# Gathered experts: all dots before all sums, and V tiles 70 to 127 as three products of split halves

## The chip, the cores and the metric

One core of one Trainium2 chip runs the whole two-block network in one launch. The metric is device microseconds of that launch; of several runs the median counts. Engines: PE (TensorE, matmuls), PEld (its weight loads), DVE (VectorE), ACT (ScalarE), POOL (GpSimd, which issues the gathers), SP (SyncE, which issues the plain loads). The sixteen DMA engines serve both queues.

## The reference, cut to what matters

The change lies in the last part, the PEER layer of the second block. Each of 512 tokens has 128 chosen experts (8 heads, 16 each) out of 16384; expert `e` has a row `peer_u[e]` and a row `peer_v[e]` of 1024 floats.

```
def chunk(args):
    hc, ec, gc = args
    u = peer_u[ec]
    a = jax.nn.gelu(jnp.einsum("ckd,cd->ck", u, hc).astype(jnp.float32)) * gc
    vv = peer_v[ec]
    return jnp.einsum("ck,ckd->cd", a.astype(vv.dtype), vv)
```

The result is added to `x`, and the sum is normalised (rmsnorm) to give the output.

## The kernel before, in words

`peer` (L1463) treats the four token tiles of 128 in two ways at once. Tiles 2 and 3 (`DT`, 256 tokens) are dense: every expert's value is computed. Tiles 0 and 1 (`GT`) are gathered: only the chosen rows are fetched.

Dense. The 16384 experts are 128 tiles of 128. `u_tile(n)` (L1721) loads a 512 KB tile of `peer_uT`, makes eight float32 matmuls with the tokens `hd` and writes gelu of the result by ACT into a slot of `big` (L1706; 94 slots `NS`, the first 50 in one tile, the other 44 in a second that `rest_of_big` makes at U tile 50; expert tile n has slot n mod 94). `gates` (L1731) multiplies slots by the gates, for expert tiles 0 to 15, 16 to 79 and 80 to 127 (`parts`) in turn: for eight tokens at a time DVE makes one-hot factors in float16 (L1759, L1760, L1764), PE multiplies them (L1748), and DVE multiplies the slots by the product (L1752). `v_tile(n)` (L1772) loads 512 KB of `peer_v` and makes four float32 matmuls (eight records in the trace: a float32 matmul here shows as two), 128 x 128 by 128 x 512, from slot n into four PSUM banks.

Gathered. `row` (L1795) is one indirect DMA issued by POOL: 128 rows of 4 KB, one for each token, into a ring of twelve buffers (`rtile`). `dots(t, s0, s1)` (L1801) gathers a column of `peer_u` and reduces its product with the tokens `h3` by one DVE instruction. `factors(t)` (L1808) makes gelu times gate of the 128 dots of each token and transposes it. `v_rows` (L1815) gathers four columns of `peer_v`; `v_sum` (L1818) copies four factors into a diagonal window by ACT (L1821) and adds the rows by eight matmuls (16 records at L1825). `last_norm(t)` (L1832) adds `x`, normalises and stores. `gather_units` (L1843) is the order of this work: dots of tile 0; then the 32 sums of tile 0 with four dots of tile 1 behind each of them; then the 32 sums of tile 1. A gather counts as one unit, so a dot is one and a sum four: 512 units in all.

The order of both. `seq` (L1875) has 256 steps: U tiles 0 to 93, then V and U tiles by turns (V0, U94, V1, ... V33, U127), then V34 to V127; so V tile n is step 94 + 2n up to n = 33 and step 128 + n from there. After each step, `fill` issues units: 1.4 a step for the first 50 steps, 2.3 from there on. `issue_after` puts the PE instructions of a unit behind the step's last matmul. DVE, ACT and POOL have no such tie: a planner lays each engine's queue in order of its own estimates of when operands are there, and on the chip each queue runs in that order. Wherever a part's V tiles begin, what is left of its gates is issued first (L1889).

`split` (L81) is used elsewhere: ACT copies a float32 tile into float32r (the high half), DVE subtracts it (the low half). `mm3` (L133) then makes three float32r matmuls: high by high, high by low, low by high.

Of the kernel before, what the change touches and what calls it, by code (L numbers as in the profile page):

```python
# [8 lines left out]
F32 = mybir.dt.float32  # L9
F32R = mybir.dt.float32r  # L10
# [10 lines left out]
S, D, NT, KD = 512, 1024, 4, 8  # L21
# [10 lines left out]
class Kern:  # L32
# [1430 lines left out]
    def peer(self):  # L1463
        nc, tc, A = self.nc, self.tc, self.A
        tt, ts, stt = nc.vector.tensor_tensor, nc.vector.tensor_scalar, nc.vector.scalar_tensor_tensor
        act = nc.scalar.activation
        GT, DT, DW = (0, 1), (2, 3), 256
        NS, NA = 94, 50
        parts = [0, 16, 80, 128]
        TB = 8  # L1470
        GS = 32768.0
        with ExitStack() as ctx:
            pb = ctx.enter_context(tc.tile_pool(name="pb", bufs=1, reuse_waits="tile"))
# [4 lines left out]
            def pu(shape=(128, 512)):  # L1478
                return pp.tile(list(shape), F32, tag="u", name=self.nm("pu"), bufs=2)

            def pw(shape=(128, 512)):
                return pp.tile(list(shape), F32, tag="w", name=self.nm("pw"), bufs=4)

            def pr(shape=(128, 512)):
                return pp.tile(list(shape), F32, tag="r", name=self.nm("pr"), bufs=2)

            def load(src, shape):

                raw = wp.tile([128] + shape, F32, tag="raw", name=self.nm("raw"))
                nc.sync.dma_start(raw[:], src)  # L1490
                return raw
# [9 lines left out]
            gp = [pb.tile([128, DW], F16, name=f"gp{j}") for j in range(2)]  # L1501
            hd = [pb.tile([128, 4, DW], F32, name=f"hd{j}") for j in range(2)]
            lctx = ctx.enter_context(ExitStack())
            lv = lctx.enter_context(tc.tile_pool(name="plv", bufs=1, reuse_waits="tile"))
            v = [lv.tile([128, 8, 2, 16], F32, name=f"pv{t}") for t in range(NT)]
            ix = [lv.tile([128, 8, 2, 16], U32, name=f"pix{t}") for t in range(NT)]
# [101 lines left out]
            with ExitStack() as c2:  # L1608
# [12 lines left out]
                for t in range(NT):  # L1621
                    tb = slice(t * 128, t * 128 + 128)
                    for j in range(2):
                        x = self.xn[t][j]
# [48 lines left out]
            def picks():  # L1673
# [9 lines left out]
                for t in DT:  # L1683
# [10 lines left out]
                    gT = wk.tile([128, 128], F32, tag="gT", name=self.nm("gT"))  # L1694
                    ts(gT[:], p[:, 2, :], GS, None, op0=OP.mult)
                    nc.vector.tensor_copy(gp[0][:, sl], gT[:])
# [9 lines left out]
            big = [bp.tile([128, NA, DW], F32, name="big")]  # L1706

            def slots(n0, n1):

                while n0 < n1:  # L1710
                    i = n0 % NS
                    b, i, w = (0, i, NA) if i < NA else (1, i - NA, NS - NA)
                    m = min(n1, n0 + w - i)
                    yield n0, m, big[b], i
                    n0 = m

            def slot(n):
                _, _, b, i = next(slots(n, n + 1))
                return b[:, i, :]

            def u_tile(n):  # L1721

                p = pu()
                raw = load(A["peer_uT"][n].rearrange("p (k e) -> p k e", k=8), [8, 128])
                for k in range(KD):
                    self.u_last = nc.tensor.matmul(p[:, :DW], raw[:, k, :], hd[k // 4][:, k % 4, :], start=k == 0,  # L1726
                                                   stop=k == KD - 1)
                self.gelu = act(slot(n), p[:, :DW], AF.Gelu_apprx_tanh)  # L1728
                self.pace = self.u_last

            def gates(n0, n1, psum):  # L1731

                w, g = n1 - n0, TB // 2

                def by2(x, t0, w):
                    return x[:, t0:t0 + TB].rearrange("p (g i) -> p g i", i=2)[:, :, None, :].to_broadcast([128, g, w, 2])

                made = []  # L1740

                def products():
                    t0, o2, og = made.pop(0)
                    p = psum([128, TB, w])
                    with tc.issue_after(self.pace.ins):
                        for i in range(TB):
                            for j in range(2):
                                nc.tensor.matmul(p[:, i, :], o2[:, i // 2, :, i % 2], og[j][:, i // 2, :, i % 2], start=j == 0,  # L1748
                                                 stop=j == 1)
                    for n, m, b, i in slots(n0, n1):  # L1750
                        b = b[:, i:i + m - n, t0:t0 + TB]
                        stt(b, p[:, :, n - n0:m - n0].rearrange("p t n -> p n t"), 1.0 / GS, b, op0=OP.mult, op1=OP.mult)  # L1752

                for t0 in range(0, DW, TB):
                    if len(made) == 2:
# [12 lines left out]
                while made:  # L1768
                    products()
                    yield  # L1770

            def v_tile(n, acc):  # L1772
                raw = load(A["peer_v_2"][n * 128:n * 128 + 128, :], [D])
                a = slot(n)
                for t, c in itertools.product(range(2), range(2)):
                    self.pace = nc.tensor.matmul(acc[t][c][:], a[:, t * 128:t * 128 + 128], raw[:, c * 512:c * 512 + 512],  # L1776
                                                 start=n == 0, stop=n == 127)

            def rest_of_big():
                lctx.close()  # L1780
                bq = ctx.enter_context(tc.tile_pool(name="pbig2", bufs=1, reuse_waits="tile"))
                big.append(bq.tile([128, NS - NA, DW], F32, name="big2"))


            ga_t = [ga.tile([128, 128], F32, name=f"ga{t}") for t in GT]
# [9 lines left out]
            def row(src, idx):  # L1795
                u = rtile("u")
                nc.gpsimd.indirect_dma_start(out=u[:], out_offset=None, in_=A[src],  # L1797
                                             in_offset=bass.IndirectOffsetOnAxis(ap=idx, axis=0))
                return u

            def dots(t, s0, s1):  # L1801
                for s in range(s0, s1):
                    u = row("peer_u_2", ei[t][:, s:s + 1])
                    nc.vector.tensor_tensor_reduce(u[:], u[:], h3[t][:], scale=1.0, scalar=0.0, op0=OP.mult, op1=OP.add,  # L1804
                                                   accum_out=ga_t[t][:, s:s + 1])
                    yield 1

            def factors(t):  # L1808
                act(ga_t[t][:], ga_t[t][:], AF.Gelu_apprx_tanh)
                tt(ga_t[t][:], ga_t[t][:], gg[t][:], op=OP.mult)  # L1810
                p = pu([128, 4, 128])
                nc.tensor.transpose(p[:, 0, :], ga_t[t][:], self.ident[:])
                act(aT[t][:].rearrange("p g r -> p (g r)"), p[:, 0, :], AF.Copy)

            def v_rows(t, r):  # L1815
                return [row("peer_v_2", eT[t][:, 32 * g + r:32 * g + r + 1]) for g in range(4)]
# [25 lines left out]

            def gather_units():  # L1843

                yield from dots(0, 0, 128)
                factors(0)
                for t in GT:
                    acc = [pr(), pr()]
                    us = v_rows(t, 0)
                    yield 4  # L1850
                    for r in range(32):
                        nx = v_rows(t, r + 1) if r < 31 else None
                        v_sum(t, r, us, acc)
                        yield 4 if r < 31 else 0
                        us = nx
                        if t == 0:
                            yield from dots(1, 4 * r, 4 * r + 4)
                    if t == 0:
                        factors(1)
                    last_norm(t, acc)  # L1860

            units = gather_units()
# [20 lines left out]
            acc, gt, todo, room = None, None, 0, 0.0  # L1883
            nbatch = DW // TB

            for j, (kind, n) in enumerate(seq):
                if kind == "v" and n == 0:
                    acc = [[pw() for _ in range(2)] for _ in range(2)]
                if kind == "v" and n in parts and gt is not None:  # L1889
                    for _ in gt:  # L1890
                        pass
                    gt = None
                if kind == "u":
                    if n == NA:
                        for _ in picks:
                            pass
                        rest_of_big()
                    if n % 3:
                        next(picks, None)
                    u_tile(n)  # L1900
                else:
                    v_tile(n, acc)
                if gt is not None:
                    todo += rate
                    while todo >= 1:
                        todo -= 1
                        next(gt, None)
                if (kind, n) in start:
                    i = start[kind, n]
                    gt, todo = gates(parts[i], parts[i + 1], pu if i else pw), 0.0  # L1910

                    rest = seq.index(("v", parts[i])) - j - 1
                    rate = (nbatch + 2) / (rest - 1)

                room = fill(room + (1.4 if acc is None and n < NA else 2.3))
# [90 lines left out]
```

## Time and profile before

| what | value |
|---|---|
| median of 3 runs | 2919.87 us (2919.39 to 2923.93) |
| the profiled execution | 2930.82 us, its span 2929.1 us |
| PE busy | 2717.2 us (93%) |
| DVE busy | 1848.5 us (63%) |
| ACT busy | 1019.7 us (35%) |
| POOL busy | 723.5 us (25%) |
| mean granted PE clock | 0.972 |
| HBM read | 736.90 MB, mean 257 GB/s over the span |
| V tiles on PE (L1776) | 1024 records, 471.4 us |
| sums on PE (L1825) | 1024 records, 126.4 us |
| dots on DVE (L1804) | 256, 311.3 us |

Busy time is added up over instructions, and PE's records overlap their neighbours by some 0.16 us; the pace of a row of matmuls is read from the distance of their starts. A group in the timeline gives start, length, engine, line, operation and, in brackets, the idle time before it with what ended it. V tile 0 starts at 2125.64 us, and the last matmul ends at 2919.7 us.

### The profile page before, as it was taken

The numbers are of one execution on the slowest core, as the hardware profiler recorded it, in microseconds if no ns is written. First come the engines' busy times: TensorE is split into PE (matmuls) and PEld (weight loads), VectorE is DVE, ScalarE is ACT, GpSimd is POOL, SyncE is SP. The second block draws the span as 40 slices with busy tenths as digits, with TensorE's granted clock in tenths as the row PEclk, the third lists the DMA queues.
The fourth block names the chain that finished last, engine by engine and source line by source line (L and its number), as shares of the span: only waits on it lengthen the run. The fifth ranks groups of instructions, "written<-read, shape, count | busy, mean of one in ns | idle before, by whom it ended". The sixth has DMA issues, their size and how long they took to land.

```text
span 2929.1 us, 38343 instructions
## 1 busy us (share of the span) xinstructions
PE 2717.2 (93%) x13730; PEld 1907.3 (65%) x13730; DVE 1848.5 (63%) x3907; ACT 1019.7 (35%) x1672; POOL 723.5 (25%) x679
## 2 busy tenths in 40 slices
PE   7999969999999879999999889989989898699998
PEld 4776757777777667766678778877745554244333
DVE  5562569998888858998535399968557522452001
ACT  5442348777777653445633332200100000000000
POOL 1000050000000110101000343566543444444440
PEclk9999979999999989999999999999999999899999
DMA  7226568989999842322222348899988899999995
GB/s 258 87 86 215 206 212 324 355 319 354 351 351 348 317 148 86 108 72 66 89 91 94 119 166 284 335 409 409 360 326 318 327 362 350 324 355 360 369 375 184
DMA packets 228689, 752.10 MB, mean 257 GB/s; under 512 B 28160, under 2 KB 28448, under 8 KB 228496
## 3 DMA queue, kind: packets, MB, share of 16 engines
q1 hardware_dynamic: 145936, 458.69, 43.7%
q0 software_dynamic: 81984, 289.89, 27.1%
q8 instruction: 109, 1.79, 0.3%
q10 hardware_dynamic: 576, 1.05, 0.1%
q14 instruction: 84, 0.69, 0.1%
HBM read 736.90 MB, written 16.81 MB: 257 GB/s over the span
## 4 chain that ended last, share of the span: by engine, by line
PE 40%; DVE 9%; DMA 7%; issue 6%; POOL 2%; ACT 1%; DVEq 0%; another core or an unknown queue 0%; POOLq 0%; SPq 0%; ACTq 0%
PE pw L1776 12%; DMA u<-in_peer_u_dram,ei 6%; PE pu L1726 4%; PE pm L136 4%; PE pm L138 4%; PE pm L137 4%; PE pr L1825 3%; POOL u L1797 2%; DVE u L1804 2%; PE pa L1305 2%; DVE cv L1236 1%; PE pu L1748 1%; PE po L1334 1%; PE pw L138 1%; PE pw L136 1%
## 5 line engine op out<-in xcount | busy, mean ns | idle before, releaser
L84 DVE TENSOR_TENSOR lo<-raw,hi 128x1024 fp32r<-128x1024 f32 (+1 forms) x580 | 624.4, 1107 | 234.3 <-ACT hi L83 214.0
L83 ACT ACTIVATE hi<-raw 128x1024 fp32r<-128x1024 f32 (+1 forms) x600 | 556.9, 952 | 445.1 <-PE pm L137 197.0
L1804 DVE CUSTOM_DVE_ANT_0 u<-u,h 128x1024 f32<-128x1024 f32 x256 | 311.3, 1226 | 305.3 <-DMA u<-in_peer_u_dram,ei 258.7
L1726 PE MATMUL pu<-hd,raw 128*128 128x256 f32 x2048 | 474.1, 390 | 17.4 <-issue 8.3
L1776 PE MATMUL pw<-raw,big 128*128 128x512 f32 x1024 | 471.4, 609 | 6.7 <-DVE big L1752 6.7
L1726 PEld LDWEIGHTS pu<-hd,raw 128*128 128x128 f32 x2048 | 394.3, 195 | 94.9 <-issue 30.2
L1776 PEld LDWEIGHTS pw<-raw,big 128*128 128x128 f32 x1024 | 191.2, 193 | 252.7 <-issue 244.0
L1797 POOL DMA_INDIRECT u<-in_peer_v_dram,eT x256 | 259.2, 1012 | 378.5 <-DVE ga L1804 210.1
L1797 POOL DMA_INDIRECT u<-in_peer_u_dram,ei x256 | 288.4, 1126 | 204.7 <-issue 54.3
L1728 ACT ACTIVATE big<-pu 128x256 f32<-128x256 f32 x128 | 48.9, 384 | 492.6 <-PE pu L1726 430.8
L137 PE MATMUL pm<-lo,xth 128*128 128x512 f32 x512 | 204.8, 400 | 6.5 <-DVE lo L84 6.5
L136 PE MATMUL pm<-hi,xth 128*128 128x512 f32 x512 | 202.1, 395 | 0.0
L138 PE MATMUL pm<-hi,xtl 128*128 128x512 f32 x512 | 201.3, 393 | 0.0
L1236 DVE SCALAR_TENSOR_TENSOR cv<-z,cols,cv 128x496 f32<-128x496 f32 (+27 forms) x240 | 167.2, 735 | 0.5
L905 POOL DMA_INDIRECT yd<-y,idx x16 | 27.6, 1726 | 540.1 <-DVE y L1009 536.6
L138 PE MATMUL pm<-hT,lo 128*128 128x512 f32 x384 | 151.2, 395 | 0.0
L136 PE MATMUL pm<-hT,hi 128*128 128x512 f32 x384 | 151.1, 394 | 0.0
L137 PE MATMUL pm<-hT,hi 128*128 128x512 f32 x384 | 151.0, 393 | 0.0
L1821 ACT ACTIVATE wz<-aT 128x4 f32<-128x4 f32 x64 | 12.8, 209 | 396.9 <-PE pr L1825 396.8
L1825 PE MATMUL pr<-u,wz 128*32 128x512 f32 x1024 | 126.4, 612 | 8.3 <-DMA u<-in_peer_v_dram,eT 8.3
L137 PEld LDWEIGHTS pm<-lo,xth 128*128 128x128 f32 x512 | 96.4, 188 | 40.3 <-DVE lo L84 19.7
L1748 PEld LDWEIGHTS <-o 128*128 128x128 f16 x1536 | 55.0, 98 | 87.5 <-DVE big L1752 43.2
(575 smaller groups left out, 4323.8 us busy)
## 6 DMA issues: line engine op xcount, KB each, us to landing
raw<-in_w_gate_dram SPq DMA_DIRECT2D x128, 512.0 KB
raw<-in_w_up_dram SPq DMA_DIRECT2D x128, 512.0 KB
raw<-in_w_down_dram SPq DMA_DIRECT2D x128, 512.0 KB
raw<-in_peer_uT_dram SPq DMA_DIRECT2D x128, 512.0 KB
raw<-in_peer_v_dram SPq DMA_DIRECT2D x128, 512.0 KB
raw<-in_w_in_dram SPq DMA_DIRECT2D x104, 256.0 KB
wa<-in_w_ada_dram SPq DMA_DIRECT2D x48, 512.0 KB
raw<-in_w_in_dram SPq DMA_DIRECT2D x28, 512.0 KB
```

The source lines that it names most:

```text
L83: return (self.nc.scalar.activation(hi, src, AF.Copy), (eng or self.nc.vector).tensor_tensor(lo, src, hi.bitcast(F32), op=OP.subtract))
L84: (eng or self.nc.vector).tensor_tensor(lo, src, hi.bitcast(F32), op=OP.subtract))
L136: mm(ps, a[0], b[0], start=first, stop=False, **kw)
L137: mm(ps, a[0], b[1], start=False, stop=False, **kw)
L138: return mm(ps, a[1], b[0], start=False, stop=last, **kw)
L1236: stt(a[:, d:], z[:, :512 - d], self.col("conv_w", k * 31 + j), a[:, d:], op0=OP.mult, op1=OP.add)
L1726: self.u_last = nc.tensor.matmul(p[:, :DW], raw[:, k, :], hd[k // 4][:, k % 4, :], start=k == 0, stop=k == KD - 1)
L1748: nc.tensor.matmul(p[:, i, :], o2[:, i // 2, :, i % 2], og[j][:, i // 2, :, i % 2], start=j == 0, stop=j == 1)
L1776: self.pace = nc.tensor.matmul(acc[t][c][:], a[:, t * 128:t * 128 + 128], raw[:, c * 512:c * 512 + 512], start=n == 0, stop=n == 127)
L1797: nc.gpsimd.indirect_dma_start(out=u[:], out_offset=None, in_=A[src], in_offset=bass.IndirectOffsetOnAxis(ap=idx, axis=0))
L1804: nc.vector.tensor_tensor_reduce(u[:], u[:], h3[t][:], scale=1.0, scalar=0.0, op0=OP.mult, op1=OP.add, accum_out=ga_t[t][:, s:s + 1])
L1825: m = nc.tensor.matmul(acc[c][32 * g:32 * g + 32, :], w[:, g, 31 - r:63 - r], us[g][:, c * 512:c * 512 + 512], start=r == 0, stop=r == 31, ...
```

## The change: what it does

`gather_units` makes the dots and factors of tile 0, then those of tile 1, and then the sums of tile 0 and of tile 1; the number of units and their pace stay. V tiles 70 to 127 are split: `v_split(n)` loads the tile and makes high and low halves of it (128 x 1024) and of slot n (128 x 256); `v_three(n)` makes `mm3` for each of the four PSUM banks, 12 float32r matmuls of 512 columns. The split of tile n + 1 is issued ahead of the products of tile n. The halves need 20 KB a partition (two buffers of each): the second `big` tile is cut in two, slots 50 to 69 and 70 to 93, and at V tile 70 the first of these is given back and the halves' pool `pv3` opened in its place. Gates of expert tiles 80 to 127 are finished one step earlier (at V79, where slot 80 is split).

```diff
+        V3 = 70
...
-                    b, i, w = (0, i, NA) if i < NA else (1, i - NA, NS - NA)
+                    b = 0 if i < NA else 1 if i < V3 else 2
+                    i, w = i - (0, NA, V3)[b], (NA, V3 - NA, NS - V3)[b]
...
+            def v_split(n):
+                raw = load(A["peer_v_2"][n * 128:n * 128 + 128, :], [D])
+                vh, vl, ah, al = [self.vp.tile([128, w], F32R, tag=x, name=self.nm(x), bufs=2)[:] for x, w in (
+                    ("vh", D), ("vl", D), ("ah", DW), ("al", DW))]
+                self.split(ah, al, slot(n))
+                self.split(vh, vl, raw[:])
+                return vh, vl, ah, al
+            def v_three(n, acc, x):
+                vh, vl, ah, al = x
+                for t, c in itertools.product(range(2), range(2)):
+                    e, d = slice(t * 128, t * 128 + 128), slice(c * 512, c * 512 + 512)
+                    self.pace = self.mm3(acc[t][c][:], (ah[:, e], al[:, e]), (vh[:, d], vl[:, d]), n == 0, n == 127)
...
-                yield from dots(0, 0, 128)
-                factors(0)
+                for t in GT:
+                    yield from dots(t, 0, 128)
+                    factors(t)
...
-                        if t == 0:
-                            yield from dots(1, 4 * r, 4 * r + 4)
-                    if t == 0:
-                        factors(1)
...
-                if kind == "v" and n in parts and gt is not None:
+                if kind == "v" and n + (n >= V3) in parts and gt is not None:
...
-                else:
-                    v_tile(n, acc)
+                elif n < V3:
+                    v_tile(n, acc)
+                else:
+                    if n == V3:
+                        self.b2ctx.close()
+                        self.vp = ctx.enter_context(tc.tile_pool(name="pv3", bufs=1, reuse_waits="tile"))
+                        nx = v_split(n)
+                    cur, nx = nx, v_split(n + 1) if n < 127 else None
+                    v_three(n, acc, cur)
```

## Rows read from the trace of the kernel before

**Rows 1.** By stage: start:end, length, busy PE PEld DVE ACT POOL, clock, DMA share, GB/s.

```profile
1900.00:1940.00 40.00, 40.00 (x187) 35.22 (x186) 26.25 (x50) 4.23 (x11) 27.82 (x22) 1.00 1.03 409
2170.00:2310.00 140.00, 122.97 (x879) 78.05 (x878) 99.03 (x224) 6.48 (x20) 54.96 (x58) 0.96 0.87 309
2464.00:2664.00 200.00, 170.05 (x898) 73.08 (x896) 92.94 (x219) 6.20 (x22) 94.44 (x96) 0.92 0.93 342
2720.00:2870.00 150.00, 150.00 (x564) 55.53 (x563) 0.00 (x0) 3.36 (x16) 67.14 (x74) 1.00 0.99 374
```

**Rows 2.** PE in order of time; the L1776 rows begin with V18, V34, V70, V82, V115.

```profile
2327.91 3.70 PE L1776 MATMUL pw<-raw,big 128*128 128x512 f32 x8
...
2463.71 7.03 PE L1776 MATMUL pw<-raw,big 128*128 128x512 f32 x16
...
2663.92 3.68 PE L1776 MATMUL pw<-raw,big 128*128 128x512 f32 x8
...
2711.25 0.56 PE L1748 MATMUL pu<-og,o 128*128 128x48 f16 x16
...
2720.66 1.92 PE L1825 MATMUL pr<-u,wz 128*32 128x512 f32 x16
2722.52 3.70 PE L1776 MATMUL pw<-raw,big 128*128 128x512 f32 x8
...
2874.80 44.90 PE L1776 MATMUL pw<-raw,big 128*128 128x512 f32 x104
```

**Rows 3.** Sums on PE by stage: PE busy (records), PEld, clock, DMA share, GB/s.

```profile
2000.00:2328.00 328.00, 30.78 (x256) 6.67 (x256) 0.96 0.92 342
2664.00:2875.00 211.00, 50.02 (x416) 10.86 (x416) 1.00 0.98 368
```

**Rows 4.** From 2000 us to the end, groups by line: dots on DVE, gathers on POOL.

```profile
L1804 DVE CUSTOM_DVE_ANT_0 u<-u,h 128x1024 f32<-128x1024 f32 x145 | 177.6, 1226 | 278.7 <-DMA u<-in_peer_u_dram,ei 235.6 <-issue 20.4 <-PE pr L1825 10.9
L1797 POOL DMA_INDIRECT u<-in_peer_u_dram,ei x138 | 138.2, 1001 | 71.8 <-issue 32.0 <-PE pr L1825 26.6 <-DVE ga L1804 7.7
```

**Rows 5.** DVE in order of time: two dots in a row, then one unit of gates.

```profile
1880.53 1.22 DVE L1804 CUSTOM_DVE_ANT_0 u<-u,h 128x1024 f32<-128x1024 f32 x1
...
1881.68 1.22 DVE L1804 CUSTOM_DVE_ANT_0 u<-u,h 128x1024 f32<-128x1024 f32 x1
...
2201.75 0.75 DVE L1752 SCALAR_TENSOR_TENSOR big<-pu,big 128x272 f32<-128x272 f32 x2
2202.41 0.68 DVE L1759 TENSOR_TENSOR o<-io,e2b 128x1024 f16<-128x1024 f16 x1
2203.01 0.75 DVE L1764 TENSOR_TENSOR og<-eq,gp 128x512 f16<-128x512 f16 x2
...
2204.83 0.42 DVE L1760 TENSOR_TENSOR eq<-io,e1b 128x512 f16<-128x512 f16 x1
```

**Rows 6.** POOL in order of time, inside and behind a stretch of dots without gaps.

```profile
1888.60 1.99 POOL L1797 DMA_INDIRECT u<-in_peer_u_dram,ei  x1 [0.30 <-issue]
...
1896.73 0.94 POOL L1797 DMA_INDIRECT u<-in_peer_u_dram,ei  x1 [0.31 <-issue]
```

**Rows 7.** First and last of 21 float32r matmuls in a row on PE, 512 columns each.

```profile
1549.73 0.40 PE L137 MATMUL pm<-oT,hi 128*128 128x512 f32 x1
...
1554.40 0.39 PE L137 MATMUL pm<-oT,hi 128*128 128x512 f32 x1
```

**Rows 8.** Groups by line and shape, whole execution: the split elsewhere, and ACT at 256 columns.

```profile
L84 DVE TENSOR_TENSOR lo<-raw,hi 128x1024 fp32r<-128x1024 f32 x432 | 519.5, 1243 | 136.7 <-ACT hi L83 127.5 <-PE pm L138 2.6 <-DMA raw<-in_w_down_dram 0.2
L83 ACT ACTIVATE hi<-raw 128x1024 fp32r<-128x1024 f32 x452 | 463.1, 1056 | 236.8 <-PE pm L138 75.1 <-DMA raw<-in_w_in_dram 44.8 <-PE pw L137 31.0
L1728 ACT ACTIVATE big<-pu 128x256 f32<-128x256 f32 x128 | 48.9, 384 | 492.6 <-PE pu L1726 430.8 <-issue 47.9 <-PE pw L1748 10.5
```

**Rows 9.** DVE at the last norm of gathered tile 1, in order of time.

```profile
2874.16 1.47 DVE L1837 TENSOR_TENSOR xe<-xe,pr 128x512 f32<-128x512 f32 x2 [161.69 <-PE pr L1825]
...
2877.16 1.41 DVE L1840 SCALAR_TENSOR_TENSOR xo<-xe,rs,gf 128x512 f32<-128x512 f32 x2
```

More of the change, by code (lines that the diff above doesn't have):

```diff
@@ L1503, in peer @@
             lctx = ctx.enter_context(ExitStack())
+            self.b2ctx = ctx.enter_context(ExitStack())
             lv = lctx.enter_context(tc.tile_pool(name="plv", bufs=1, reuse_waits="tile"))
@@ L1780, in rest_of_big @@
                 lctx.close()
-                bq = ctx.enter_context(tc.tile_pool(name="pbig2", bufs=1, reuse_waits="tile"))
-                big.append(bq.tile([128, NS - NA, DW], F32, name="big2"))
+                bq = ctx.enter_context(tc.tile_pool(name="pbig3", bufs=1, reuse_waits="tile"))
+                b3 = bq.tile([128, NS - V3, DW], F32, name="big3")
+                bq = self.b2ctx.enter_context(tc.tile_pool(name="pbig2", bufs=1, reuse_waits="tile"))
+                big.extend([bq.tile([128, V3 - NA, DW], F32, name="big2"), b3])
             ga_t = [ga.tile([128, 128], F32, name=f"ga{t}") for t in GT]
```

## The prediction

> **What bounds the kernel now.** I read the slices of the page first: up to some 1900 us nothing touches the change, so only the last 1000 us count. Then I cut these into stages by busy time [rows 1]: the reader is to see that one engine after the other binds. At 1900 to 1940 us the transfers are full: 409 GB/s, and no stretch shows more. At 2170 to 2310 us nothing is full: DVE 99.0 of 140 us, PE 123.0, 309 GB/s. The engines wait for each other there: DVE's queue holds dots that wait for their rows, gates stand behind these dots, and PE's products behind the gates; PE's clock falls to 0.92 from 2464 to 2664 us, where it waits most. From 2720 us on PE works without a gap, at 374 GB/s, not far below 409. The timeline of PE [rows 2] gives the places: V18 at 2328, V34 at 2464, V70 at 2664, V115 (the first behind all sums) at 2875, end of matmuls at 2919.7. Waiting dots explain much of it: of the time from 2000 us on DVE stood 235.6 us for rows of `peer_u` [rows 4].
>
> **What moves.** 512 units at 1.4 a step for 50 steps and 2.3 behind them end at step 50 + 442/2.3 = 242 (V115), as rows 2 show, and so they do afterwards. The dots now end at unit 256: step 50 + 186/2.3 = 131, about V18. So from 2000 us to V18 there are 64 more dots and 16 fewer sums; from V18 on 64 sums, 0.575 a step, and no dot. On POOL the gathers are as many and change only their order. I go stage by stage, against the profiled execution.
>
> **2000 us to V18, now 328 us.** DVE: 145 dots are left at 2000 us [rows 4], 1.15 us each in a row [rows 5]: 167 us. The gates of tiles 16 to 79 are 32 units of 0.66 + 0.60 + 0.67 + 0.33 = 2.26 us [rows 5]; their range of slots now crosses two borders, one piece more of about 0.2 us: 79 us. The first part's units, about 21 left (an estimate), some 1.3 us each since all but one operation shrink: 27 us. Sum 273 us. Transfers: 138 gathers [rows 4] and about 66 loads of 0.524 MB, 107 MB at 409 GB/s [rows 1]: 262 us. PE loses the 16 sums, 30.8 us [rows 3]. So PE, DVE and the transfers are loaded about alike. It can't be under 273; if DVE keeps the 71% busy share of 2170 to 2310 us [rows 1], it is 273/0.71 = 385. I take half of the PE time freed, 328 - 15 = 313: the ring of twelve holds dots alone, which DVE frees at once, where now it also holds rows that wait for a sum. Change: -15 (-55 to +57).
>
> **The first sum.** PE's transposes for the factors stand behind the last dot, and the first four rows of `peer_v` must land; today sums are under way by then. 0 to 15 us; I take 8.
>
> **V18 to V34, now 136 us.** 31 steps of 3.45 us (44.90/104 x 8, [rows 2]; I take a U tile alike) are 107, 18 sums of 1.86 us (distance 2720.66 to 2722.52) 33: 140, and a few waits: 144. Change +8: this stage pays for sums that stood earlier.
>
> **V34 to V70, now 200 us.** 36 V tiles are 124 us, 21 sums 39, 27 products of gates at 0.5 [rows 2] 14: 177. What stops PE today goes: 30 us idle and a clock of 0.92 [rows 1], behind dots that wait for rows. Next late would be transfers: 0.575 x 4 + 1 = 3.3 of them a step are 1.73 MB, 4.2 us at 409 GB/s, under PE's 4.9. I take 180. Change -20 (-23 to 0).
>
> **Entering V70.** The halves' pool lies where slots 50 to 69 were, so the first split waits for V69: ACT 0.38 and 1.06 us, DVE 1.24 [rows 8], then PE. 0 to 4 us; I take 3.
>
> **V70 to V115, now 211 us.** Twelve float32r matmuls at (1554.40 - 1549.73)/20 = 0.2335 us [rows 7] are 2.80 us for 3.45: 45 x 2.80 = 126, 26 sums [rows 3] 48, eight products 4: 178 us for PE. Transfers: 45 loads and 104 gathers, 78 MB: 191 us at 409 GB/s, 209 at 374; up to 16 of the 149 stand in the buffers already, 20 us less. I take 186, nearer to the full rate. Change -25 (-33 to 0). The cover of the split: ACT 0.38 + 1.06, DVE about 0.45 + 1.24 (128 x 256 on DVE isn't in the trace; ACT's 0.38 and a quarter of 1.24 bound it). That is 1.7 us of DVE a tile, and DVE has almost nothing else there; SP's loads wait for `raw` buffers, which the split now frees a tile earlier than PE did. But with two buffers the split of tile n + 1 starts when PE leaves n - 1 and must be done one tile later: ACT's 1.06, then DVE's 1.24 and three signals, some 2.7 us against 2.80 plus one matmul until the low half is read. It fits barely; without that cover each tile would take 0.3 us more, 4 us behind the sums and less before them, where a sum gives 1.86 us of room.
>
> **The last 13 tiles and the end.** 13 x 0.65 = 8 us less. Ahead of them the norm of gathered tile 1 now stands on DVE and ACT before the next splits: its DVE work runs from 2874.2 to 2878.6 [rows 9], longer than one tile. 0 to 6 us; I take 4. The norms of tiles 2 and 3 stay.
>
> **Sum.** -15 + 8 + 8 - 20 + 3 - 25 - 8 + 4 = -45 us. The profiled execution took 2930.8 us and would take 2886; the median of the runs shown, 2919.9, is 11 us lower, so I forecast 2875.
>
> **A rule that speaks against it.** Inside a stretch of dots without gaps a gather holds POOL for 1.99 us, behind it 0.94 [rows 6]. The Trainium skill ("SBUF — State Buffer", section "Who interferes with whom") says that a DVE instruction with two SBUF inputs contends with a GpSimd instruction that reads SBUF, the later one being blocked until the first is done. The trace agrees inside that stretch, but 138 gathers took 1.00 us on average [rows 4], though DVE was busy most of the time.
>
> **The rivals.**
> 1. Transfers hide the products: from V70 on the bytes flow at the 374 GB/s of today [rows 1], and what PE saves becomes waiting. Then 209 instead of 186 us: 2875 + 23 = 2898. For it: the DMA share there is already 0.99. Against: 409 at 1900 us.
> 2. Slower: the dots' stretch is held by DVE's queue. With 64 more dots among the gates and 71% busy it takes 385 us instead of 313: 2875 + 72 = 2947. It decides once V18 starts later than 2000 + 313 + 45 = 2358 us. For it: products wait for gates behind dots, and PE's clock drops to its lower level behind such waits. Against: the ring then holds nothing that waits for PE.
> 3. POOL binds there: 138 gathers at 1.99 + 0.30 [rows 6] are 316 us, and with the waits of a chain (313 is 1.15 x 273) 362: 2875 + 49 = 2924, no change. Against: gaps of DVE make POOL fast again.
> 4. The dots' stretch runs at DVE's bound, 273 us: 2875 - 40 = 2835.
> That the change doesn't do what it says: the planner may lay gates ahead of dots as it does now; it moves single waits and belongs to 2.
>
> **How the numbers follow.** Forecast 0.64, with its own range 2852 to 2896 (stages' ends that don't all fall together); rival 1 0.15; 2 0.08; 3 0.06; 4 0.07. The range 2836 to 2910 holds the forecast, rival 1 and most of 4. A measurement here tells 0.2% from nothing, 2914 to 2926. Faster: forecast, 1 and 4, 0.86, with the edge of 1 taken off and that of 3 added; same 0.06, most of rival 3; slower 0.08.
>
> **What would show it.** V18 near 2313 us and the dots over by then; 18 sums between V18 and V34; no PE gap over a few us from V34 to V70, clock near 1.00; 12 records of some 0.39 us at 0.2335 us distance for each tile from V70 on, V70 to V115 in 178 to 191 us with transfers near 400 GB/s; the last 13 tiles at 2.8 us, DVE's low halves landing just ahead of PE. The prediction is wrong if V18 comes after 2358 us, if PE waits for DVE or ACT in most tiles from V70 on, or if gathers there hold each sum by more than 1 us.

## The result and the profile after

The changed kernel takes 2857.31 us (median of 4 runs, 2854.90 to 2859.73) beside 2921.77 us for the kernel before in the same runs: ratio 0.978, 95% interval 0.9763 to 0.9797. The forecast was 2875 us, 18 us too high, inside its range. The profiled execution took 2854.9 us, its span 2853.2 us, at a mean PE clock of 0.978.

The profiled executions differ by 2930.82 - 2854.90 = 76 us, the medians by 64.5: the execution shown of before lies 9.1 us above its median, that of after 2.4 us below. The forecast of -45 us was for the medians as well, so against them it is 19.5 us short, against the profiled executions 31.

The stages of after, by start:end, length, busy time of PE, PEld, DVE, ACT and POOL, clock, DMA share and GB/s. The first row is the window of [rows 1]; the next ones run from 2000 us to V18, from there to V34, to V70, to V115, and to the last matmul:

```profile
2170.00:2310.00 140.00, 125.96 (x781) 82.95 (x780) 123.69 (x291) 6.57 (x18) 65.10 (x58) 0.95 0.90 326
2000.00:2292.00 292.00, 260.58 (x1737) 194.47 (x1735) 266.65 (x618) 18.58 (x52) 180.48 (x141) 0.95 0.97 369
2292.00:2440.00 148.00, 146.72 (x658) 78.82 (x659) 9.12 (x22) 9.93 (x34) 73.50 (x76) 1.00 1.00 386
2440.00:2618.00 178.00, 177.67 (x1025) 73.69 (x1023) 54.04 (x151) 8.40 (x30) 81.43 (x88) 1.00 0.97 360
2618.00:2806.00 188.00, 180.70 (x1068) 112.79 (x1068) 87.21 (x128) 68.09 (x115) 99.72 (x99) 1.00 1.03 407
2806.00:2843.00 37.00, 36.01 (x159) 29.05 (x156) 23.33 (x31) 17.46 (x30) 0.00 (x0) 1.00 0.53 181
```

The first row against [rows 1]: in the same window DVE goes from 99.0 to 123.7 us busy. The third and fourth rows have what [rows 1] lacked from 2464 to 2664 us: a clock of 1.00, and PE busy nearly all the time. The fifth has 407 GB/s, where [rows 1] have 374.

PE in order of time, the rows that answer to [rows 2]: V18 with the first sum behind it; V70; V115; and the only wait in the tiles behind V115 that is over half a microsecond:

```profile
2292.19 3.70 PE L1794 MATMUL pw<-raw,big 128*128 128x512 f32 x8 [1.45 <-DMA raw<-in_peer_v_dram]
...
2300.61 1.91 PE L1845 MATMUL pr<-u,wz 128*32 128x512 f32 x12
2302.45 0.33 PE L1832 MATMUL pu<-ident,ga 128*128 128x128 f32 x1
...
2618.72 1.20 PE L136 MATMUL pw<-vh,ah 128*128 128x512 f32 x4 [1.05 <-ACT vh L83]
...
2806.33 0.50 PE L136 MATMUL pw<-vh,ah 128*128 128x512 f32 x1
2806.67 0.40 PE L137 MATMUL pw<-vl,ah 128*128 128x512 f32 x1
2806.91 0.40 PE L138 MATMUL pw<-vh,al 128*128 128x512 f32 x1
...
2813.89 0.50 PE L137 MATMUL pw<-vl,ah 128*128 128x512 f32 x1 [0.99 <-DVE vl L84]
```

V0 begins at 2120.8 us (2125.6 before). Between the marks, in us:

| from | before | after | forecast of the change | measured |
|---|---|---|---|---|
| 2000 us to V18 | 327.9 | 292.2 | -15 | -35.7 |
| V18 to V34, first sum included | 135.8 | 147.7 | +8 +8 | +11.9 |
| V34 to V70 | 200.2 | 178.8 | -20 | -21.4 |
| V70 to V115 | 210.9 | 187.6 | +3 -25 | -23.3 |
| V115 to the end of the last matmul | 44.9 | 37.1 | -8 +4 | -7.8 |
| sum | | | -45 | -76.3 |

Part of the first two rows is scatter of single executions. The run products_alone below has the old order too, and slightly more work ahead of V70 than the kernel before; its profiled execution began V18 at 2321.9 us and V70 at 2651.7, 6.0 and 12.2 us ahead of the execution of before that is shown. Against it the first row of the table is -29.7 us and the second +19.0.

From 2000 us to the end, groups by line and shape of DVE (busy us, mean ns, then idle before them and what ended it): the dots, and the two low halves of the split:

```profile
L1824 DVE CUSTOM_DVE_ANT_0 u<-u,h 128x1024 f32<-128x1024 f32 x144 | 173.6, 1220 | 18.0 <-DMA u<-in_peer_u_dram,ei 17.3
L84 DVE TENSOR_TENSOR vl<-raw,vh 128x1024 fp32r<-128x1024 f32 x58 | 71.3, 1229 | 23.3 <-ACT vh L83 23.3
...
L84 DVE TENSOR_TENSOR al<-big,ah 128x256 fp32r<-128x256 f32 x58 | 24.8, 427 | 87.6 <-ACT ah L83 87.3
```

The wait of dots for their rows has gone from 235.6 us [rows 4] to 17.3. The same stretch on POOL, gathers by the tensor that they read:

```profile
L1817 POOL DMA_INDIRECT u<-in_peer_v_dram,eT x256 | 256.8, 1003 | 244.0 <-PE pr L1845 156.6 <-issue 39.8 <-DMA u<-in_peer_v_dram,eT 17.5
L1817 POOL DMA_INDIRECT u<-in_peer_u_dram,ei x137 | 174.2, 1272 | 110.6 <-DVE ga L1824 69.6 <-issue 24.4 <-DVE og L1767 7.7
```

### The profile page after: what moved, and what is told of

It is laid out like the page before. It is cut to its first block, busy times and chain, and to the rows that moved or that the text cites. A ratio compares the mean times of both kernels' runs of the same rounds, so it can differ in the third digit from the quotient of the medians.

```text
span 2853.2 us, 39121 instructions
## 1 busy us (share of the span) xinstructions
PE 2669.4 (94%) x13962; PEld 1942.4 (68%) x13962; DVE 1937.4 (68%) x4055; ACT 1099.8 (39%) x1788; POOL 758.9 (27%) x679
## 3 DMA queue, kind: packets, MB, share of 16 engines
q10 hardware_dynamic: 576, 1.05, 0.1%
## 4 chain that ended last, share of the span: by engine, by line
PE 37%; DVE 13%; DMA 11%; issue 2%; POOL 1%; ACT 1%; DVEq 0%; SPq 0%; POOLq 0%; ACTq 0%
DMA u<-in_peer_u_dram,ei 7%; PE pw L1794 7%; PE pm L136 4%; PE pm L138 4%; PE pm L137 4%; PE pr L1845 4%; DVE u L1824 3%; PE pu L1729 3%; PE pw L136 2%; DMA u<-in_peer_v_dram,eT 2%; PE pw L137 2%; PE pw L138 2%; PE pa L1305 2%; DVE cv L1236 1%; PE po L1334 1%
## 5 line engine op out<-in xcount | busy, mean ns | idle before, releaser
L1817 POOL DMA_INDIRECT u<-in_peer_u_dram,ei x256 | 326.1, 1274 | 243.3 <-DVE ga L1824 97.8
L1794 PE MATMUL pw<-raw,big 128*128 128x512 f32 x560 | 263.8, 612 | 17.0 <-DMA raw<-in_peer_v_dram 13.0
L1767 DVE TENSOR_TENSOR og<-eq,gp 128x128 f16<-128x128 f16 (+2 forms) x192 | 59.0, 332 | 253.3 <-PE pu L1751 253.1
L1794 PEld LDWEIGHTS pw<-raw,big 128*128 128x128 f32 x560 | 102.7, 193 | 141.6 <-issue 120.4
L136 PEld LDWEIGHTS pm<-hi,xth 128*128 128x128 f32 x512 | 96.4, 188 | 21.1 <-ACT xth L83 0.2
```

The costliest lines, as they stand in the source:

```text
L136: mm(ps, a[0], b[0], start=first, stop=False, **kw)
L1767: tt(o[:], eq[:], by2(gp[j], t0, w), op=OP.mult)
```

## Experiments

Each was timed beside the kernel before; medians of 4 or 5 runs, if nothing else is said. Marks are starts in the profiled execution. Beside the first four the kernel before took 2922.21 us, beside the next four 2921.43.

### Each part of the change alone

order_alone is the kernel before with the new order of units:

```diff
-                yield from dots(0, 0, 128)
-                factors(0)
+                for t in GT:
+                    yield from dots(t, 0, 128)
+                    factors(t)
...
-                        if t == 0:
-                            yield from dots(1, 4 * r, 4 * r + 4)
-                    if t == 0:
-                        factors(1)
```

> The kernel before with the new order of gather_units and nothing else. My theory: order and products are two separate gains. The changed kernel reached V18 36 us earlier than the kernel before, lost 12 of it to V34, won 21 to V70; all of that is the order. So 2922 - 45 = 2877 us, V70 about 45 us earlier, V70 to V115 about 208 us as before. Rival: the order only moves work between stages and the products make the gain: 2900 us or more.

Measured: 2880.32 us, ratio 0.9865 (0.9847 to 0.9883). Its stages from 2000 us to V18 and from V70 to V115, with columns as above:

```profile
2000.00:2287.00 287.00, 261.04 (x1761) 195.73 (x1759) 266.01 (x589) 18.57 (x52) 181.04 (x141) 0.96 0.98 378
2613.00:2824.00 211.00, 211.00 (x889) 80.49 (x888) 12.92 (x37) 4.93 (x23) 90.25 (x99) 1.00 0.98 367
```

products_alone has the split and the old order (the same lines of `gather_units`, the other way round, on the changed kernel).

> The changed kernel with the old order of gather_units. My theory: V70 to V115 23 us shorter, the last 13 tiles 8 us shorter, nothing else: 2922 - 31 = 2891 us. Rival (the transfers hide the products as long as sums are under way): only the last 13 tiles gain, 2914 us. Rival (the two help each other): over 2900 us here and over 2885 us with the order alone.

Measured: 2889.15 us (2883.6 to 2894.04), ratio 0.9895 (0.9871 to 0.9919). Its stages from V34 to V70 and from V70 to V115:

```profile
2451.00:2652.00 201.00, 171.82 (x898) 73.24 (x897) 92.75 (x221) 7.80 (x26) 98.15 (x96) 0.92 0.94 342
2652.00:2838.00 186.00, 180.71 (x1068) 112.52 (x1067) 86.12 (x125) 67.12 (x113) 96.54 (x98) 1.00 1.02 406
```

The two parts work in different stages. The order gives all of the gain up to V70 and leaves V70 to V115 at 211 us; the products leave V34 to V70 at 201 us with the clock at 0.92, and bring V70 to V115 from 211 to 186. So the order gives 42 us and the products 33, 75 together. The change gives 64.5, but the product of the two ratios, 0.9865 x 0.9895 = 0.9761, can't be told from 0.978 within the intervals; whether the parts take something from each other stays open. The marks show more than 42 us, because the execution of before that is shown is a long one: V70 comes 51 us earlier in order_alone than in it, and 39 us earlier than in products_alone.

### Half of the dots left among the sums

half_of_the_dots_late is the changed kernel with dots 64 to 127 of tile 1 put among the sums of tile 0, two behind each:

```diff
-                for t in GT:
-                    yield from dots(t, 0, 128)
-                    factors(t)
+                yield from dots(0, 0, 128)
+                factors(0)
+                yield from dots(1, 0, 64)
...
+                        if t == 0:
+                            yield from dots(1, 64 + 2 * r, 66 + 2 * r)
+                    if t == 0:
+                        factors(1)
```

> The changed kernel, but only the first 64 dots of tile 1 stand ahead of the sums; two more follow behind each sum of tile 0. Theory 1: DVE binds the dots' stretch (267 of its 292 us busy) and all-dots-first overshoots; some 43 dots, 49 us of DVE, leave the stretch, V18 comes 10 to 15 us earlier, total 2840 to 2850 us. Theory 2: what the change removed is the queueing of dots and sum rows in one ring of twelve and one POOL queue; with both kinds mixed again DVE waits for rows as before, 2865 to 2885 us.

Measured: 2868.95 us, ratio 0.9823 (0.9801 to 0.9845), some 12 us above the changed kernel. Of the theories in the expectation the one by which dots that stand among rows of sums cost time is borne out; the other fell: V18 came at 2302.7 us, 10.5 us later than in the changed kernel and not earlier. The waits of DVE from 2000 to 2300 us (total us, times, longest), first this kernel, then products_alone and the kernel before (all dots of tile 1 among sums), then the changed one (none):

```profile
DVE u L1824 <- DMA u<-in_peer_u_dram,ei: 56.6, 36, 8.2
```

```profile
DVE u L1824 <- DMA u<-in_peer_u_dram,ei: 91.3, 30, 9.4
```

```profile
DVE u L1804 <- DMA u<-in_peer_u_dram,ei: 92.1, 28, 9.1
```

```profile
DVE u L1824 <- DMA u<-in_peer_u_dram,ei: 17.3, 30, 1.6
```

Waits of at most 1.6 us in a row of dots become waits of up to 9.4 us when sums stand between, and their total follows the share of dots mixed in. In the stage from V34 to V70 it shows on PE too: 196 us with a clock of 0.95, between the 201 at 0.92 of products_alone and the 178 at 1.00 of after:

```profile
2440.00:2636.00 196.00, 174.91 (x948) 74.31 (x947) 79.84 (x198) 7.95 (x27) 91.57 (x95) 0.95 0.95 351
```

### Do transfers or PE bind from V70 on?

half_rows_tile_1 leaves out half of the rows of `peer_v` of tile 1: two are gathered for each sum, and each is used twice. PE's work stays the same.

```diff
-                return [row("peer_v_2", eT[t][:, 32 * g + r:32 * g + r + 1]) for g in range(4)]
+                us = [row("peer_v_2", eT[t][:, 32 * g + r:32 * g + r + 1]) for g in range(4 if t == 0 else 2)]
+                return us if t == 0 else us + us
```

> The changed kernel with half of the peer_v gathers of tile 1 left out (two rows a sum, each used twice), so 64 of 128 gathers fewer from about V59 on; PE's work is the same. Theory: from V70 to V115 transfers (407 GB/s) and PE (181 of 188 us busy) bind together, so the stage falls from 188 to about 179 us and the total by 8 to 11 us, 2847 us. Rival A (transfers alone bind there): the stage falls towards PE's floor and the total by 15 us or more. Rival B (the split's chain of ACT and DVE binds): no change, 2857 us.

Measured: 2845.83 us, ratio 0.9747 (0.9729 to 0.9764). V70 to V115:

```profile
2615.00:2796.00 181.00, 180.90 (x1069) 112.87 (x1069) 86.99 (x128) 67.50 (x115) 44.23 (x46) 1.00 0.81 270
```

With a third less data the stage takes 181 us instead of 187.6, and PE has no gap left. In the changed kernel PE and the transfers are thus loaded almost alike: what the transfers add is near 7 us, and 6.4 us of that are five sums that wait for their rows:

```profile
PE pr L1845 <- DMA u<-in_peer_v_dram,eT: 6.4, 5, 2.1
```

Of the 11.5 us between the medians the stage explains these 7. V18 comes 3.9 us earlier than in the profiled execution of after, where the edit changes nothing; that is scatter again.

slower_pace_from_70 gives the transfers longer: fewer units a step from V70 on, so that sums run beside the last tiles, where the changed kernel moves only 181 GB/s.

```diff
-                room = fill(room + (1.4 if acc is None and n < NA else 2.3))
+                room = fill(room + (1.4 if acc is None and n < NA else 1.95 if kind == "v" and n >= V3 else 2.3))
```

> The changed kernel with 1.95 units a step from V70 on instead of 2.3, so that the sums end some seven steps later. Theory: from V70 to V115 transfers and PE bind together (PE idle 7 of 188 us), and behind it the transfers are half idle (181 GB/s); spread evenly PE's waits go: 2857 - 6 = 2851 us, gathers no longer waited for by sums. Rival: PE's own work sets the end, 217 us busy of 225 from V70 on, and the waits only move: 2857 us.

Measured: 2847.84 us, ratio 0.9747 (0.9729 to 0.9766). V70 to V115, and from there to the last matmul:

```profile
2620.00:2794.00 174.00, 172.49 (x1004) 111.24 (x1005) 86.51 (x126) 65.90 (x113) 88.02 (x86) 1.00 1.01 395
2794.00:2838.00 44.00, 43.94 (x220) 30.38 (x219) 23.90 (x32) 18.90 (x32) 9.09 (x12) 1.00 0.80 319
```

From V70 to the end of the last matmul it is 218.6 us instead of 224.7: four sums go behind V115, PE's gaps ahead of it shrink from 7.3 us to 1.5, and the end moves data at 319 GB/s. These 6 us are what the stages show; the medians differ by 9.5.

### Does DVE bind the stretch of dots?

gates_parts_at_70 puts the border of the second and third part of the gates at expert tile 70. That makes the units of the second part smaller, and no piece of the slots crosses the border of the buffers at 70 any more.

```diff
-        parts = [0, 16, 80, 128]
+        parts = [0, 16, 70, 128]
...
-                if kind == "v" and n + (n >= V3) in parts and gt is not None:
+                if kind == "v" and n + (n > V3) in parts and gt is not None:
```

> The changed kernel with the gates' second part ending at expert tile 70 instead of 80 (so no range of gates crosses the new border of the big tiles, and 54 columns instead of 64 stand in the dots' stretch). Theory: DVE binds from 2000 us to V18 (267 of 292 us busy); it has 32 x 0.46 = 15 us less there, so V18 comes about 10 us earlier and the total is 2847 us. Rival: transfers (262 us of work there) and PE bind alike, so nothing or under 4 us comes of it.

Measured: 2842.63 us, ratio 0.9739 (0.972 to 0.9759). From 2000 us to V18:

```profile
2000.00:2274.00 274.00, 255.09 (x1734) 192.36 (x1733) 255.06 (x582) 18.19 (x51) 179.79 (x139) 0.97 1.01 390
```

DVE has 11.6 us less to do there, PE 5.5 us, and the stage is 18 us shorter, where the theory had some 10. PE's waits for loads of `raw` from 2000 to 2300 us (total us, times, longest), in the changed kernel and here:

```profile
PE pw L1794 <- DMA raw<-in_peer_v_dram: 13.0, 4, 6.8
```

```profile
PE pw L1794 <- DMA raw<-in_peer_v_dram: 1.4, 2, 0.8
```

So the stage moves with the gates' work, and the rival by which under 4 us would come of it fell. But the edit takes work from DVE and from PE, and 18 us is more than DVE's 11.6: on PE's side it is 5.5 us of work and some 12 of waits for loads. That DVE's work alone sets the stage is not shown. The stage is near three limits by now: DVE and PE busy 93% of it, the transfers at a share of 1.01. Some of the gain is paid back behind it: the third part's gates now cover 58 expert tiles instead of 48 and stand ahead of V70, and V34 to V70 takes 185.6 us instead of 178.8.

parts_and_pace has both edits.

> Both edits, the parts' border at 70 and 1.95 units from V70 on. If they are independent, 2841 us; if the transfers bind behind both, no better than the better one of them.

Measured: 2834.27 us, ratio 0.9701 (0.9684 to 0.9718), 23 us under the changed kernel and the best version run. Its stage from V70 to V115 and the end:

```profile
2609.00:2778.00 169.00, 168.81 (x890) 108.48 (x891) 75.75 (x91) 66.17 (x113) 85.58 (x86) 1.00 1.02 405
2778.00:2823.00 45.00, 44.74 (x223) 30.75 (x221) 23.88 (x33) 19.45 (x33) 11.08 (x13) 1.00 0.80 317
```

The two edits add, as far as the medians tell: 14.7 us for the parts and 9.5 for the pace make 24.2, and 23.0 were measured.

### Why does mixing cost? Two rings

Rows of dots and rows of sums share one ring of twelve buffers: a row that waits for its sum keeps a buffer from a dot. If that is the cause, the old order should lose its waits when each kind has a ring of its own. two_rings_old_order is the kernel before with four buffers for dots and eight for sums:

```diff
-                return gr.tile([128, D], F32, tag="u", name=self.nm(nm), bufs=12)
+                return gr.tile([128, D], F32, tag="u", name=self.nm(nm), bufs=8)
...
-                u = rtile("u")
+                d = src == "peer_u_2"
+                u = gr.tile([128, D], F32, tag="d" if d else "u", name=self.nm("u"), bufs=4 if d else 8)
```

> The kernel before, old order, but dots and sum rows in rings of their own, four and eight of the same twelve buffers. Theory 1: what made DVE wait for rows in the old order is the shared ring (a dot's gather needs the buffer of a sum that PE hasn't made); then DVE's wait for rows of peer_u from 2000 us on, 236 us before, falls below 120 and the total by 15 to 30 us. Theory 2: it is POOL's one queue, in which gathers of sums that wait for a buffer stand ahead of gathers of dots, whatever the ring; then the wait stays near 236 us and the total within 10 us of 2922, or above where four buffers are too few for dots alone.

Measured: 2958.46 us beside 2921.43, ratio 1.0133 (1.0112 to 1.0153). V0 is 54 us late: while only dots run, four buffers seem too few (from 1700 us to V0 DVE waits 98.2 us for rows, before 65.5). From 2000 us on DVE's wait for rows of dots is 145.1 us (for 163 dots that are left there, where it was 145), neither under the 120 of the first theory nor near the 236 of the second. From V0 to V70 it takes 503.5 us, though, for 538.3 before and 497.9 after. So this run spoiled one stage and mended another, and decides nothing alone. two_rings_from_tile_1 lets the dots of tile 0 use both rings:

```diff
...
-            def row(src, idx):
-                u = rtile("u")
+            def row(src, idx, tag="u"):
+                u = gr.tile([128, D], F32, tag=tag, name=self.nm("u"), bufs=4 if tag == "d" else 8)
...
-                    u = row("peer_u_2", ei[t][:, s:s + 1])
+                    u = row("peer_u_2", ei[t][:, s:s + 1], "u" if 128 * t + s < 128 and s % 3 else "d")
```

> The kernel before, old order; the dots of tile 0 use all twelve buffers by turns, the dots of tile 1 only a ring of four and the sum rows one of eight. V0 then comes at 2125 us as before, and what follows shows the rings alone. Theory 1 (the shared ring makes dots wait for sums): from V0 to V70 500 to 510 us instead of 538, total 2885 to 2900 us. Theory 2 (POOL's one queue does it, whatever the ring): V0 to V70 530 us or more, total 2910 us or more.

Measured: 2917.91 us (10 runs) beside 2923.06 (13), ratio 0.9984 (0.9972 to 0.9996). From V18 to V34 and from V34 to V70:

```profile
2341.00:2487.00 146.00, 134.12 (x529) 77.72 (x528) 43.45 (x71) 7.69 (x26) 73.35 (x71) 0.94 0.96 369
2487.00:2649.00 162.00, 162.00 (x899) 70.55 (x898) 53.67 (x151) 5.97 (x21) 50.37 (x56) 1.00 0.83 291
```

V34 to V70 becomes as free of waits as a new order makes it (162 us, PE full, clock 1.00; it holds 13 sums, as before, where the changed kernel has 21). But V0 comes 12 us later, V18 to V34 takes 146 us for 136, and DVE waits 171.6 us for rows of dots where it waited 235.6. From V0 to V70 it takes 510.7 us, at the edge of the first theory's range, while the total is the second's. The ring is a part of the cause, not the whole. half_late_two_rings asks the same of half_of_the_dots_late, with two rings from dot 64 of tile 1 on:

```diff
+                    u = row("peer_u_2", ei[t][:, s:s + 1], "u" if 128 * t + s < 192 and s % 3 else "d")
```

> half_of_the_dots_late with the two rings from dot 64 of tile 1 on. Theory 1: without the shared ring the later dots cost DVE no more waits than they save it work, so it comes out at or under the changed kernel's 2857 us instead of 2869. Theory 2: 2869 us again, or above.

Measured: 2880.54 us, ratio 0.9851 (0.9828 to 0.9873), 12 us slower than with one ring, though DVE's wait for rows of dots falls from 228.2 to 123.8 us. V18 comes at 2325 us instead of 2303, but V34 to V70 takes 171 us instead of 196, so that V70 is reached at 2636 us in both. What is lost is lost behind it, where no dot is left: with eight buffers instead of twelve for the sums V70 to V115 takes 202 us instead of 186, and PE waits 15.2 us there for rows of `peer_v` instead of 5.1. A ring that is split leaves each kind with too few buffers.

The trace of the kernel before has one more clue. From 2000 us on POOL stood 378.5 us ahead of the gathers for sums, and what ended this was mostly a dot:

```profile
L1797 POOL DMA_INDIRECT u<-in_peer_v_dram,eT x256 | 259.2, 1012 | 378.5 <-DVE ga L1804 210.1 <-PE pr L1825 100.0 <-issue 35.4
```

Ahead of the gathers for dots a sum ended only 26.6 us of POOL's idle time [rows 4]. So a sum's gather that waits for the buffer of a dot, with the next dots' gathers behind it in POOL's one queue, is at least as likely a cause as a row of a sum that keeps a buffer from a dot. No run here separates these from the bare number of buffers, and that stays open.

## Why the prediction came out as it did

**2000 us to V18: the step that was mis-sized.** Forecast 313 us, measured 292. The work was right: 273 us of DVE, and 266.7 were measured. The step that failed is "I take half of the PE time freed": it left 40 us of waits, and there were 25, with DVE busy 91% of the stage against 71% in the window of [rows 1]. The mechanism named beside it held, that a ring with dots alone is freed at once: dots waited 17.3 us from 2000 to 2300 us, for 92.1 before, and with half of the dots late it was 56.6. No run gives a reason for half of PE's freed time; the stage came out as DVE's work plus 25 us of waits, and as 255 plus 19 in gates_parts_at_70, though that run takes work from PE too. Some 5 us of the stage were won already ahead of V0. This one term is 21 of the 31 us by which the sum was short of the profiled difference; some 6 of the 21 are the scatter named below the table.

**The first sum and V18 to V34.** Forecast 152 us in all, measured 147.7, and that this is near is luck. The first sum starts 8.4 us behind V18, but PE has other work until then: it is busy 146.7 of 148 us, so the 8 us that were taken for waiting did not occur. In their place PE had more to do than the forecast's 140 us. The stage has 32 steps and not 31 (16 V tiles and 16 U tiles), each some 3.54 us long, and 17 sums:

```profile
2307.15 3.72 PE L1729 MATMUL pu<-hd,raw 128*128 128x256 f32 x16
2310.71 3.60 PE L1794 MATMUL pw<-raw,big 128*128 128x512 f32 x8
2314.24 1.92 PE L1845 MATMUL pr<-u,wz 128*32 128x512 f32 x16
```

That makes 113 + 32 = 145 us.

**V34 to V70.** Forecast 180, measured 178.8: PE's gaps go, the clock rises to 1.00, and 21 sums are in it, as the step had it. order_alone has the same without the products, so this is the order's doing. How the 200 us of before divide is shown by two_rings_from_tile_1, which has the same 13 sums there and takes 162 us without a gap: of the 38 us more, 30 were waits, and some 8 the slower pace at a mean granted clock of 0.92.

**V70 to V115.** With the entry 189 forecast, 187.6 measured. The entry is one wait of 1.05 us for the high half. PE was given 178 us and had 180.7; the transfers were given 409 GB/s and had 407. They were nearly level, as half_rows_tile_1 shows. The step "nearer to the full rate" held. The 374 GB/s of the old stage were no limit of the transfers: PE was busy 150 of 150 us there [rows 1] and asked for no more.

**The split's cover.** It held. ACT's halves of a tile in the last stretch, from the timeline, columns as for PE:

```profile
2818.76 0.42 ACT L83 ACTIVATE ah<-big 128x256 fp32r<-128x256 f32 x1 [1.35 <-PE pw L137]
2819.08 1.05 ACT L83 ACTIVATE vh<-raw 128x1024 fp32r<-128x1024 f32 x1
2821.48 0.42 ACT L83 ACTIVATE ah<-big 128x256 fp32r<-128x256 f32 x1 [1.35 <-PE pw L137]
```

and DVE's:

```profile
2821.93 0.43 DVE L84 TENSOR_TENSOR al<-big,ah 128x256 fp32r<-128x256 f32 x1 [0.54 <-ACT ah L83]
2822.88 1.23 DVE L84 TENSOR_TENSOR vl<-raw,vh 128x1024 fp32r<-128x1024 f32 x1 [0.52 <-ACT vh L83]
2824.65 0.43 DVE L84 TENSOR_TENSOR al<-big,ah 128x256 fp32r<-128x256 f32 x1 [0.54 <-ACT ah L83]
```

The period is 2.72 us on both, PE's pace for a tile (12 x 0.227), and ACT waits for PE in each: PE leads and the chain of halves follows. The low half that begins at 2822.88 is done at 2824.11, and PE's first product that reads it begins at 2824.45: 0.34 us to spare where no sum helps. The low half of the slot took 0.43 us, the estimate 0.45.

**The end.** Forecast -8 +4, measured -7.8. The tiles give 13 x (3.45 - 2.72) = 9.5 us. The norm of tile 1 cost less than the 4 us taken: PE waited 0.99 us, once, in the row at 2813.89. Its additions on DVE began at 2807.2 us and its last product there ended at 2812.7, so the next low half came late by that much only.

**The rivals.** Transfers at 374 GB/s: 407 were measured. DVE's queue: its condition was V18 behind 2358 us, and it came at 2292. Those two fell, and so did the third as a bound: gathers for dots took 1.27 us on POOL, not 1.99, and POOL was busy 180 of 292 us. The direction of the rule that was cited ("SBUF — State Buffer" in the Trainium skill, section "Who interferes with whom") agrees, since the mean was 1.00 in the old order [rows 4] and is 1.17 with half the dots late, but that the port is the reason no run here isolates; for the 37 us that this adds (137 x 0.27) POOL had room. The fourth rival, DVE's bound, lies nearest: 273 us plus 19.

## What to carry to other kernels

Work that is freed at once and work that holds its buffers until another engine takes it should not take turns in one ring and one queue: all of the first kind and then all of the second gave 42 us here with the same work, and dividing the ring instead (four and eight buffers, from tile 1 on) gave 5. When a chain of waits goes, the busy share of the stage that had it is no guide (71% of DVE here, 91% afterwards); the fullest engine's whole load plus some waits was nearer (267 + 25 us, and 255 + 19 in gates_parts_at_70). Where two resources are level at one stage and idle at the next, move work over the border: a pace of 1.95 instead of 2.3 units gave 6 us by the stages and 9.5 by the medians.

## What was not expected of the hardware

Transfers held 407 GB/s for 188 us with two thirds of the bytes in gathers. The prediction had it from 40 us of the kernel before [rows 1], but the trace of before shows the same rate for 150 us in a row, which speaks against rival 1 more than the prediction saw:

```profile
1900.00:2000.00 100.00, 89.19 (x527) 77.12 (x525) 75.07 (x154) 9.15 (x24) 72.18 (x55) 0.95 1.03 409
2000.00:2050.00 50.00, 45.98 (x320) 39.35 (x321) 36.87 (x89) 4.79 (x17) 31.47 (x25) 0.93 1.03 409
```

Float32r matmuls of 512 columns ran at a distance of 0.227 us in the V tiles, for 0.2335 in the older row [rows 7]. And near the end of the stretch of dots PE waited 13.0 us, four times, for loads of `peer_v` tiles, the longest 6.8 us, while the transfers moved only 311 GB/s (2200 to 2300 us). The transfers were not full, then. The load behind the longest of these waits was issued only at 2262.97 us, as PE ended a U tile (2262.94), and PE's wait for it ended at 2270.90; SP's queue had stood for buffers that PE gives back. Why PE gave them back late there no run shows.
